# A softmax-times-V kernel: each row's product made for its two heads apart, in two halves of the PSUM partitions

## The chip, the cores and the metric

The kernel runs on one core of one Trainium2 chip. The metric is the device time of one launch in microseconds; a comparison uses the median of several launches.

## The reference

```python
scores: (8, 12, 1024, 1024) float32     # batch, heads, queries, keys
v:      (8, 12, 1024, 64)  float32
attn = exp(scores - max(scores, -1)); attn = attn / (sum(attn, -1) + 1e-8)
out  = matmul(attn, v)                   # (8, 12, 1024, 64) float32
```

The scores are 403 MB and are read once; everything else is small beside them.

## The kernel before, in words

There are 96 heads (batch times heads). One pass of the hardware loop takes `AHEAD` = 4 of them, so the loop runs 24 times. Two heads make a tile of the loop body (`T` = 2, `K` = 2 tiles in a body). A tile is `s_bufs[k]`, 128 partitions by `R` = 16 rows by 1024 scores in float32 (8 MB): partitions 0 to 63 hold the first head, 64 to 127 the second, and each partition has 16 neighbouring queries of its head. "Row r" below means the 128 queries (64 of each head) that stand at place r of all partitions.

For every tile the function `heads` goes through its 16 rows:

- ACT (line 377) takes exp of two rows at a time (one at a time in the last half of the second tile, where `late` holds), without subtracting the maximum, and writes float16 into `p_nat` (eight buffers of two rows, which is one whole tile).
- PE (line 390) transposes the row with 8 matmuls against the identity, one for each chunk of 128 keys, into `psT` in PSUM (two buffers of two rows).
- DVE (line 402, or 398 where `late` holds) copies `psT` to `pt` in SBUF.
- PE (line 152, function `finish`) makes the product with V: 8 matmuls, one for each chunk, which accumulate. The stationary operand is the 128x128 block of `pt` (64 queries of the one head, 64 of the other). The moving operand is V of both heads side by side with a column of ones, 130 columns in all (`M`). So all 128 queries are multiplied with both heads' V, and half of what comes out is not used.
- For each group of `G` = 3 rows (one PSUM bank, `psO`), DVE (function `normalise`) takes the reciprocal of the column of ones' result (line 132) and multiplies the 64 results with it, once for each head (line 140, partitions 0 to 63 and 64 to 127), into `out_bufs[k]`. The sixteenth row is a group of its own, so there are six groups in a tile.

`finish` runs `LAG` = 3 rows behind the transposes: the order on PE is written out by `in_line` as transposes of row r, product of row r-3, transposes of row r+1 and so on. At the end of a body the remaining products follow, and then `judge`: four small DVE instructions over the sums seen so far, one small matmul (line 297) and a cast. It decides whether a general path must run at the very end (it does not here). `watch_v` (line 259) is one DVE reduction over V in each body.

All transfers stand in one queue on SP in an order of their own (`queue`): the next body's first tile (`load_first`, behind ACT's reading of this body's first tile), the first tile's output, the next body's second tile, the second tile's output, and V two bodies ahead (behind GpSimd's spreading of V, line 248). In the last body the second tile is loaded in smaller pieces, and the function `end` stores the output in two parts.

Every weight load and every matmul of the body increments one semaphore of PE when it is done; DVE, ACT, GpSimd and SP wait on its value.

Of the kernel before, what the change touches and what calls it, by code (L numbers as in the profile page):

```python
# [12 lines left out]
ALU = mybir.AluOpType  # L13
# [13 lines left out]
def kernel(  # L27
# [6 lines left out]
    nc = tc.nc  # L34
    P = 128

    B, H, SQ, SK = scores.shape
    Bv, Hv, SKv, D = v.shape
# [2 lines left out]
    assert SQ % P == 0 and SK % P == 0  # L41
    C = SK // P
    EB = 2
    G = 3
    LAG = 3
    AHEAD = 4
    Q = P // AHEAD
# [5 lines left out]
    T = 2  # L53
    K = AHEAD // T
    W = P // T
    R = SQ // W
    N = D + 2
    M = T * N - 2
    GROUPS = -(-R // G)

    sc_rows = scores.rearrange("b h (j r) k -> (b h j) r k", j=W).rearrange(
        "(m x) r k -> m x r k", x=P
# [13 lines left out]
    vones = const_pool.tile([P, K, C, T, N], FP16, name="vones")  # L76
    nc.vector.memset(vones[:, :, :, :, D:N], 1.0)  # L77

    def buffers(pool, count, shape, dtype, name):
        return [pool.tile(shape, dtype, name=f"{name}{k}") for k in range(count)]  # L80
# [5 lines left out]
    out_bufs = buffers(sb_pool, K, [P, R, D], FP32, "out_sb")  # L86
    small_pool = ctx.enter_context(tc.tile_pool(name="small", bufs=1))
    seen = small_pool.tile([P, 1 + K * R + 1], FP32, name="seen")
# [7 lines left out]
    def take(bufs):  # L96
        k = turn.get(id(bufs), 0)
        turn[id(bufs)] = k + 1
        return bufs[k % len(bufs)]

    pending = []
# [3 lines left out]
    def after(a, b):  # L105

        tc.add_manual_dep(
            a.ins,
            b.ins.name,
            mybir.DependencyInfo(mybir.DependencyClass.NoSync, mybir.DependencyReason.DATA),  # L110
            reason="order",
        )

    def in_line(op):

        if line:
            after(op, line[-1])
        line.append(op)
# [4 lines left out]
            after(dma, queued[-1])  # L123
        queued.append(dma)

    def invert(k, st, g):

        rows = min(G, R - g * G)
        psO = st["psO"][g][:, 0 : rows * M].rearrange("p (g m) -> p g m", m=M)
        at = 1 + k * R + g * G  # L130
        recip = seen[:, at : at + rows].rearrange("p (g o) -> p g o", o=1)
        nc.vector.reciprocal(out=recip, in_=psO[:, :, D : D + 1])  # L132
        return psO, recip

    def normalise(k, st, g):
        psO, recip = invert(k, st, g)
        rows = min(G, R - g * G)
        for t in range(T):
            part = slice(t * W, (t + 1) * W)
            nc.vector.tensor_tensor(  # L140
                out=out_bufs[k][part, g * G : g * G + rows, :],
                in0=psO[part, :, t * N : t * N + D],
                in1=recip[part].to_broadcast([W, rows, D]),
                op=ALU.mult,
            )

    def finish(u):

        n0, k, r, pt, st = u
        g, i = r // G, r % G  # L150
        for c in range(C):
            product = nc.tensor.matmul(  # L152
                out=st["psO"][g][:, i * M : (i + 1) * M],
                lhsT=pt[:, c * P : (c + 1) * P],
                rhs=vones[:, k, c].rearrange("p t n -> p (t n)")[:, 0:M],
                start=(c == 0),
                stop=(c == C - 1),
            )
            in_line(product)
        if i == G - 1 or r == R - 1:  # L160
            normalise(k, st, g)
        if r == R - 1 and k < K - 1:
            spread_v(k)
            store(n0, k)

    def store(n0, k):

        to = out_rows.rearrange("(m x) y -> m x y", x=P)[bass.ds((n0 + T * k) // T, 1)]
        to = to.rearrange("o x y -> (o x) y")
        send(nc.sync.dma_start(out=to, in_=out_bufs[k][:].rearrange("x r d -> x (r d)")))  # L170

    def send(dma):
        for other in stores:
            apart(dma, other)
            apart(other, dma)
        apart(dma, dma)
        stores.append(dma)
        queue(dma)

    def end():  # L180

        cut = (GROUPS - 2) * G
        for a, b in ((0, cut), (cut, R)):
            send(
                nc.sync.dma_start(
                    out=out_rows[(BH - T) * W : BH * W, a * D : b * D],
                    in_=out_bufs[K - 1][:, a:b].rearrange("x r d -> x (r d)"),
                )
            )
# [8 lines left out]
    def rewrite(buf, op):  # L198


        others = writers.setdefault(buf.name, [])
        for other in others:
            apart(op, other, "readers in between")
            apart(other, op, "readers in between")
        apart(op, op, "readers in between")
        others.append(op)

    def other_bank(tile, bank, op):

        for other in users.setdefault((tile.name, 1 - bank), []):  # L210
            apart(op, other, "banks are disjoint")
            apart(other, op, "banks are disjoint")
        users.setdefault((tile.name, bank), []).append(op)
# [30 lines left out]
    def spread_v(k):  # L244

        for t in range(T):
            for s in range(S):
                spread = nc.gpsimd.tensor_copy(  # L248
                    out=vones[s * Q : (s + 1) * Q, k, :, t, 0:D].rearrange(
                        "i (h l) d -> i h l d", l=L  # L250
                    ),
                    in_=v_sb[(k * T + t) * Q : (k * T + t + 1) * Q, :, s],
                )
                for watch in watches:
                    apart(spread, watch, "products in between")

    def watch_v(behind):

        watch = nc.vector.tensor_reduce(  # L259
            out=most,  # L260
            in_=vones[:, :, :, :, 0:D].rearrange("p k c t d -> p k (c t) d"),
            axis=mybir.AxisListType.XYZ,
            op=ALU.max,
            apply_absolute_value=True,
        )
        after(watch, behind)
        watches.append(watch)
        for bound, op in ((V_MIN, ALU.is_ge), (V_MAX, ALU.is_le)):
            nc.vector.scalar_tensor_tensor(  # L269
                out=fits, in0=most, scalar=bound, in1=fits, op0=op, op1=ALU.mult  # L270
            )
# [9 lines left out]
    def judge(bank):  # L281
# [12 lines left out]
        )  # L294
        cell = bank[0:1, G * M : G * M + 1]
        in_line(
# [70 lines left out]
    def heads(n0):  # L367

        for k in range(K):
            st = dict(psO=[take(psO_bufs) for g in range(GROUPS)])  # L370
            for r in range(R):
                late = k == K - 1 and r >= R // 2
                if r % EB == 0:
                    p_nat, psT2, pt2 = take(p_bufs), take(psT_bufs), take(pt_bufs)
                    rows = 1 if late else EB
                    for g in range(0, EB, rows):
                        exp = nc.scalar.activation(  # L377
                            out=p_nat[:, g : g + rows, :].rearrange(
                                "p r (x v) -> p x r v", v=Q * L
                            ),  # L380
                            in_=s_bufs[k][:, r + g : r + g + rows, :].rearrange(
                                "p r (i x l) -> p x (r i) l", i=Q, l=L
                            ),
                            func=EXP,
                        )
                        rewrite(p_nat, exp)
                p_row = p_nat[:, r % EB, :].rearrange("p (h q l) -> p h l q", q=P, l=L)
                psT, pt = psT2[:, r % EB, :], pt2[:, r % EB, :]
                for c in range(C):
                    turned = nc.tensor.transpose(  # L390
                        out=psT[:, c * P : (c + 1) * P],
                        in_=p_row[:, c // L, c % L, :],
                        identity=ident16[:],
                    )
                    in_line(turned)
                    other_bank(psT2, r % EB, turned)
                if late:
                    copy = nc.vector.tensor_copy(out=pt, in_=psT)  # L398
                    rewrite(pt2, copy)
                    other_bank(psT2, r % EB, copy)  # L400
                elif r % EB == EB - 1:
                    copy = nc.vector.tensor_copy(out=pt2[:], in_=psT2[:])  # L402
                    rewrite(pt2, copy)
                if k == 0 and r == R // 2 - 1:
                    watch_v(copy)
                if r == R - 1 and k < K - 1:
                    load_first(n0)
                pending.append((n0, k, r, pt, st))
                if len(pending) > LAG:
                    finish(pending.pop(0))  # L410
        while pending:
            finish(pending.pop(0))
        last(n0)
        judge(st["psO"][-1])
# [51 lines left out]
```

## Time and profile before

| | |
|---|---|
| median of 3 runs | 1070.41 us (1070.23 to 1070.44) |
| the profiled execution: its time, its span | 1069.46 us, 1067.5 us |
| PE matmul busy | 793.6 us (74%), 12312 instructions |
| DVE busy | 768.8 us (72%), 1539 instructions |
| ACT busy | 737.3 us (69%) |
| transfers | 453.06 MB, mean 424 GB/s |
| one body of the loop, from the trace | 43.6 us |

Busy times of PE are of overlapping instructions, so the sum of a group says little of its pace; the starts in the timeline do. A name such as `L152` is line 152 of the kernel. PE stands for matmuls, PEld for weight loads.

### The profile page before, as it was taken

To read this page: it belongs to the slowest core of one execution; us is meant where nothing else is said; L and a number is where in the kernel's file an instruction comes from. 1 tells how busy PE (TensorE), PEld (TensorE's weight loads), DVE (VectorE), ACT (ScalarE), POOL (GpSimd) and SP (SyncE) were. 2 spreads that over 40 slices of the span, in tenths; PEclk is the share of its full clock that TensorE was granted. 3 is DMA by queue.
4 is the path that set the end of the run, shared out by engine and by line. 5 is a ranking of instruction groups with operands and counts; after the bars stand their busy time and mean duration, and the time that the engine had idled before them with its cause. 6 is when DMAs were issued, how large, how long until landed. Compare 5 with 4: busy or idle time off the path is not lost.

```text
span 1067.5 us, 32791 instructions
## 1 busy us (share of the span) xinstructions
PE 793.6 (74%) x12312; PEld 757.7 (71%) x12312; DVE 768.8 (72%) x1539; ACT 737.3 (69%) x504; POOL 239.2 (22%) x399
## 2 busy tenths in 40 slices
PE   2578768786786777867878668776786777866887
PEld 2578668686686776867768668776686777866877
DVE  1578767696686866867769667785686866867788
ACT  3567568666686576856867668667686586756893
POOL 3031131211311203113121131221311303113121
PEclk9889889898898988989989889898898988989899
DMA  9999999999999999999999999999999999999993
GB/s 393 441 438 413 422 462 413 452 413 431 453 413 452 426 419 449 417 433 446 440 425 449 425 423 452 413 428 456 413 452 413 431 453 413 452 410 434 432 429 151
DMA packets 18580, 453.06 MB, mean 424 GB/s; under 512 B 2064, under 2 KB 2192, under 8 KB 8720
## 3 DMA queue, kind: packets, MB, share of 16 engines
q1 hardware_dynamic: 18576, 452.99, 98.6%
q8 instruction: 4, 0.07, 0.0%
HBM read 637.53 MB, written 25.17 MB: 621 GB/s over the span
## 4 chain that ended last, share of the span: by engine, by line
DMA 58%; ACT 27%; issue 6%; PE 3%; PEld 2%; DVE 2%; ACTq 1%; SPq 0%; PEldq 0%; DVEq 0%
DMA s_nat<-in_scores_dram 58%; ACT p_nat L377 26%; PE psO L152 1%; PEld L390 1%; PE psT L390 1%; DVE pt L402 1%; PEld L152 1%; ACTq L377 1%; DVE most L259 0%; ACT L377 0%; DVE pt L398 0%; SPq L219 0%; ACTq L423 0%; DVE seen L132 0%; DVE out_sb L140 0%
## 5 line engine op out<-in xcount | busy, mean ns | idle before, releaser
L377 ACT ACTIVATE p_nat<-s_nat 128x2048 f16<-128x2048 f32 (+1 forms) x480 | 706.5, 1557 | 118.9 <-PE psO L152 42.5
L390 PE MATMUL psT<-ident,p_nat 128*128 128x128 f16 x6144 | 505.4, 232 | 166.2 <-ACT p_nat L377 166.2
L390 PEld LDWEIGHTS <-p_nat 128*128 128x128 f16 x6144 | 425.1, 118 | 176.0 <-ACT p_nat L377 176.0
L402 DVE COPY pt<-psT 128x2048 f16<-128x2048 f16 x288 | 352.4, 1224 | 261.5 <-PE L390 165.2
L152 PE MATMUL psO<-vones,pt 128*128 128x130 f16 x6144 | 486.6, 223 | 62.9 <-DVE fits L269 40.4
L152 PEld LDWEIGHTS <-pt 128*128 128x128 f16 x6144 | 387.8, 99 | 84.7 <-DVE pt L402 55.6
L248 POOL CAST vones<-v_sb 32x512 f16<-32x512 f32 x392 | 238.5, 608 | 813.4 <-PE psT L390 318.6
L140 DVE TENSOR_TENSOR out_sb<-psO,seen 64x192 f32<-64x192 f32 (+1 forms) x576 | 191.8, 333 | 18.0
L377 ACT ACT_TABLE_LOAD x24 | 30.8, 1283 | 195.4 <-DMA s_nat<-in_scores_dram 178.5
L398 DVE COPY pt<-psT 128x1024 f16<-128x1024 f16 x192 | 123.5, 685 | 2.3
L259 DVE TENSOR_REDUCE most<-vones 128x1 f32<-128x2048 f16 x24 | 54.9, 2286 | 0.7
L132 DVE RECIPROCAL seen<-psO 128x3 f32<-128x3 f32 (+1 forms) x288 | 49.3, 171 | 2.8 <-PE L390 1.4
L297 PE MATMUL psO<-vones,right 128*1 128x1 f16 x24 | 3.9, 164 | 41.0 <-DVE right L292 41.0
L297 PEld LDWEIGHTS <-right 128*1 128x1 f16 x24 | 1.9, 79 | 45.3 <-DVE right L292 45.3
L301 DVE CAST count<-psO 1x1 int32<-1x1 f32 x24 | 3.5, 146 | 6.2 <-PE psO L297 6.2
L269 DVE SCALAR_TENSOR_TENSOR fits<-most,fits 128x1 f32<-128x1 f32 x48 | 7.4, 155 | 0.0
L289 DVE SCALAR_TENSOR_TENSOR part<-seen,fits 128x1 f32<-128x1 f32 x24 | 5.3, 220 | 0.8
L285 DVE TENSOR_REDUCE seen<-seen 128x1 f32<-128x33 f32 x24 | 4.5, 188 | 0.8
L292 DVE SCALAR_TENSOR_TENSOR right<-seen,part 128x1 f16<-128x1 f32 x24 | 3.9, 162 | 0.8
L286 DVE TENSOR_REDUCE seen<-seen 128x1 f32<-128x33 f32 x24 | 4.2, 177 | 0.0
L77 DVE MEMSET vones<- 128x64 f16 x1 | 0.1, 112 | 0.8 <-PEq L450 0.8
L74 DVE CAST ident<-ident 128x128 f16<-128x128 f32 x1 | 0.2, 227 | 0.4 <-POOL ident masks.py:199 0.4
(8 smaller groups left out, 1.1 us busy)
## 6 DMA issues: line engine op xcount, KB each, us to landing
s_nat<-in_scores_dram SPq DMA_DIRECT2D x50, 4096.0 KB, 18.7
v_sb<-in_v_dram SPq DMA_DIRECT2D x24, 1024.0 KB, 22.2
out_dram<-out_sb SPq DMA_DIRECT2D x47, 512.0 KB, 16.8
s_nat<-in_scores_dram SPq DMA_DIRECT2D x2, 2048.0 KB, 22.8
s_nat<-in_scores_dram SPq DMA_DIRECT2D x1, 1536.0 KB, 27.5
s_nat<-in_scores_dram SPq DMA_DIRECT2D x3, 512.0 KB, 20.8
s_nat<-in_scores_dram SPq DMA_DIRECT2D x1, 1024.0 KB
s_nat<-in_scores_dram SPq DMA_DIRECT2D x47, 28.4
```

The source lines that it names most:

```text
L132: nc.vector.reciprocal(out=recip, in_=psO[:, :, D : D + 1])
L140: nc.vector.tensor_tensor(out=out_bufs[k][part, g * G : g * G + rows, :], in0=psO[part, :, t * N : t * N + D], in1=recip[part].to_broadcas ...
L152: product = nc.tensor.matmul(out=st["psO"][g][:, i * M : (i + 1) * M], lhsT=pt[:, c * P : (c + 1) * P], rhs=vones[:, k, c].rearrange("p t ...
L248: spread = nc.gpsimd.tensor_copy(out=vones[s * Q : (s + 1) * Q, k, :, t, 0:D].rearrange("i (h l) d -> i h l d", l=L), in_=v_sb[(k * T + t) ...
L259: watch = nc.vector.tensor_reduce(out=most, in_=vones[:, :, :, :, 0:D].rearrange("p k c t d -> p k (c t) d"), axis=mybir.AxisListType.XYZ, ...
L269: nc.vector.scalar_tensor_tensor(out=fits, in0=most, scalar=bound, in1=fits, op0=op, op1=ALU.mult)
L289: nc.vector.scalar_tensor_tensor(out=part, in0=seen[:, n + 1 : n + 2], scalar=1.0, in1=fits, op0=ALU.is_le, op1=ALU.mult)
L297: nc.tensor.matmul(out=cell, lhsT=right[:], rhs=vones[:, 0, 0, 0, D : D + 1], start=True, stop=True)
L377: exp = nc.scalar.activation(out=p_nat[:, g : g + rows, :].rearrange("p r (x v) -> p x r v", v=Q * L), in_=s_bufs[k][:, r + g : r + g + ro ...
L390: turned = nc.tensor.transpose(out=psT[:, c * P : (c + 1) * P], in_=p_row[:, c // L, c % L, :], identity=ident16[:],)
L398: copy = nc.vector.tensor_copy(out=pt, in_=psT)
L402: copy = nc.vector.tensor_copy(out=pt2[:], in_=psT2[:])
```

## The change

The product of a row is made by 16 matmuls instead of 8: for each chunk and each head one, with 64 columns of `pt` as stationary operand and that head's own 65 columns of V and ones as moving operand. The first head's result goes to PSUM partitions 0 to 63, the second's to 64 to 127. The tiles that the build gives to these instructions are 128x64 at columns 0 and 64 of the array; transposes keep 128x128. A row now takes 65 columns of PSUM instead of 130, so a bank holds four rows (`G` = 4), a tile has four groups, and one multiplication of 128 partitions by 256 elements normalises a group. Near the end of a body (`late`, the last two rows) the products run two rows behind instead of three. In the built program the body has 256 weight loads and 256 matmuls for transposes as before, and 512 and 512 instead of 256 and 256 for products; the order of DVE, ACT, GpSimd and SP instructions is the same but for the fewer normalisations.

```diff
-    G = 3
+    G = 4
...
-    M = T * N - 2
-    GROUPS = -(-R // G)
+    M = D + 1
+    GROUPS = R // G
...
-    def invert(k, st, g):
-
-        rows = min(G, R - g * G)
-        psO = st["psO"][g][:, 0 : rows * M].rearrange("p (g m) -> p g m", m=M)
+    def normalise(k, st, g):
+
+        psO = st["psO"][g][:, 0 : G * M].rearrange("p (g m) -> p g m", m=M)
         at = 1 + k * R + g * G
-        recip = seen[:, at : at + rows].rearrange("p (g o) -> p g o", o=1)
+        recip = seen[:, at : at + G].rearrange("p (g o) -> p g o", o=1)
         nc.vector.reciprocal(out=recip, in_=psO[:, :, D : D + 1])
-        return psO, recip
-
-    def normalise(k, st, g):
-        psO, recip = invert(k, st, g)
-        rows = min(G, R - g * G)
-        for t in range(T):
-            part = slice(t * W, (t + 1) * W)
-            nc.vector.tensor_tensor(
-                out=out_bufs[k][part, g * G : g * G + rows, :],
-                in0=psO[part, :, t * N : t * N + D],
-                in1=recip[part].to_broadcast([W, rows, D]),
-                op=ALU.mult,
-            )
+        nc.vector.tensor_tensor(
+            out=out_bufs[k][:, g * G : (g + 1) * G, :],
+            in0=psO[:, :, 0:D],
+            in1=recip.to_broadcast([P, G, D]),
+            op=ALU.mult,
+        )
...
         for c in range(C):
-            product = nc.tensor.matmul(
-                out=st["psO"][g][:, i * M : (i + 1) * M],
-                lhsT=pt[:, c * P : (c + 1) * P],
-                rhs=vones[:, k, c].rearrange("p t n -> p (t n)")[:, 0:M],
-                start=(c == 0),
-                stop=(c == C - 1),
-            )
-            in_line(product)
-        if i == G - 1 or r == R - 1:
+            for t in range(T):
+                product = nc.tensor.matmul(
+                    out=st["psO"][g][t * W : (t + 1) * W, i * M : (i + 1) * M],
+                    lhsT=pt[:, c * P + t * W : c * P + (t + 1) * W],
+                    rhs=vones[:, k, c, t, 0:M],
+                    start=(c == 0),
+                    stop=(c == C - 1),
+                )
+                in_line(product)
+        if i == G - 1:
             normalise(k, st, g)
...
-        cut = (GROUPS - 2) * G
+        cut = (GROUPS - 1) * G
...
-                if len(pending) > LAG:
+                while len(pending) > (LAG - 1 if late and r >= R - EB else LAG):
                     finish(pending.pop(0))
```

## The prediction, made before the changed kernel ran

> **What bounds the kernel now.** I read the page first, then the windows of one body and of the end, then the timeline of one body, then the list of waits, and last the trace's own record of semaphore updates.
>
> ```profile
> q1 hardware_dynamic: 18576, 452.99, 98.6%
> L390 PE MATMUL psT<-ident,p_nat 128*128 128x128 f16 x6144 | 505.4, 232 | 166.2 <-ACT p_nat L377 166.2
> L152 PE MATMUL psO<-vones,pt 128*128 128x130 f16 x6144 | 486.6, 223 | 62.9 <-DVE fits L269 40.4
> 505.10:548.70 43.60, 32.54 (x513) 30.98 (x513) 32.00 (x64) 30.77 (x22) 10.97 (x19) 0.90 1.00 433
> 1048.00:1068.00 20.00, 13.31 (x226) 12.72 (x223) 14.79 (x38) 3.62 (x4) 4.78 (x8) 0.93 0.16 62
> ```
>
> The first three are lines of the page, the last two windows (length, busy time of PE, PEld, DVE, ACT, POOL, clock, DMA share, GB/s). For a body of 43.6 us the DMA engines are never idle: transfers set the period, and PE, DVE and ACT each have about 11 us to spare. Only in the last 20 us are the transfers over; there the time is that of the chain through PE and DVE.
>
> ```profile
> 513.42 0.61 PE L390 MATMUL psT<-ident,p_nat 128*128 128x128 f16 x8
> 513.87 0.62 PE L152 MATMUL psO<-vones,pt 128*128 128x130 f16 x8
> 514.16 1.22 DVE L402 COPY pt<-psT 128x2048 f16<-128x2048 f16 x1 [0.84 <-PE psO L152]
> 514.33 0.61 PE L390 MATMUL psT<-ident,p_nat 128*128 128x128 f16 x8
> ...
> 502.13 0.64 PE L152 MATMUL psO<-vones,pt 128*128 128x130 f16 x8 [0.74 <-DVE pt L398]
> ...
> 504.48 0.17 PE L297 MATMUL psO<-vones,right 128*1 128x1 f16 x1 [1.71 <-DVE right L292]
> ...
> 508.36 3.70 PE L390 MATMUL psT<-ident,p_nat 128*128 128x128 f16 x32 [3.72 <-ACT p_nat L377]
> ```
>
> In the timeline a row takes PE 0.91 us (513.42 to 514.33): 8 transposes 0.45, 8 products 0.46, that is 55 to 57 ns for a weight load and its matmul. A body has 32 rows, 29.1 us. Then PE waits, for `judge` (1.71) and for the next tile (3.72).
>
> ```profile
> DVE pt L402 <- PE L152: 48.8, 35, 11.3
> DVE pt L402 <- PE psO L152: 42.9, 45, 1.8
> ```
>
> These are the lines of the list of waits that I find odd. The copy at L402 needs transposes (L390), yet it is mostly released while products run; the copy at 514.16 starts 0.13 us after the transposes' modelled end. The record of semaphore updates says why. PE's semaphore gets 24,629 increments, one from each of the 12,312 weight loads and 12,312 matmuls and a few more. Of the 24,628 distances between them, 23,208 are exactly 30 ns, and none is shorter. In busy stretches 36 instructions end in a microsecond and 33 increments come; the increments fall up to 22 behind the ends, and DVE starts 23 to 24 ns after an increment, not after an end. So PE's done signals go out one by one, 30 ns each. A row now has 32 of them, 0.96 us, just over PE's 0.91; a body 1026 of them, 30.8 us, well under 43.6.
>
> **The change, part by part.**
>
> *Signals.* A row gets 16 transposing instructions (8 loads, 8 matmuls) and 32 for the product, each with its increment: 48 x 30 ns = 1.44 us. A body has 512 + 1024 + 2 = 1538, and 1538 x 0.030 = 46.1 us, more than the 43.6 us of the transfers. This alone makes PE's signals the bound, whatever the matmuls cost up to 1.44 us a row.
>
> *PE itself.* No instruction of 64 stationary columns stands in the trace. Below: the moving columns halve (65 for 130), so a load and matmul take 27.5 ns and the row stays at 0.91. Above: they take 55 ns, as the fullest ones do, 16 x 55 = 0.88, and the row is 1.33. The array also changes between tiles of 128 and 64 columns twice a row. A change costs nothing if it is hidden; at most it waits for the last matmul (about 220 ns from start to end, less the usual 55) and a load (97 ns), 0.26 us. So a row takes PE 0.91 to 1.86 us. I take 1.15 to 1.4, in the middle, below the signals' 1.44, and keep the upper end for the range.
>
> [...]
>
> *DVE.* The multiplications of a tile go from 10 of 64x192 (355 ns) and 2 of 64x64 (222) to 4 of 128x256. The two rows give 133 ns for 128 elements more, so 64x256 would be about 422; all partitions work at once. With 6 and 4 reciprocals of 0.17: 5.0 us becomes 2.4 a tile, 5.2 us saved a body. It lies beside PE and the transfers and is worth nothing in the steady bodies. PE's wait of 1.7 us a body behind `watch_v` (40.4 us over 24 bodies, put down to DVE fits in the L152 line above) goes too: at 1.44 us a row, the signals of two rows (2.88) outlast the reduction (2.29), and the copy behind it is needed only two rows later.
>
> *Lag.* One product moves ahead of the last transposes. At the end of a body it covers the last copy (0.69 us; 0.74 of wait at 502.13 is gone). This I count as part of the signal stream.
>
> *What follows at the body's end.* Signals stop from the last product's increment (502.80) to the next body's first (now 508.49). What stays of that when PE no longer waits for a tile: reciprocal, multiplication, four small ones and the small matmul to 504.66 (1.86; the new multiplication costs 0.42 for 0.47), PE's branch rows to 505.58 (0.92), then the first load's 0.13: 2.9 us. Then four rows of transposes (64 signals, 1.92) stand against the first two rows' 0.96, copy 1.24 and about 0.2 of starts, so 0.45 us more. Together 3.4.
>
> So a body takes 46.1 + 3.4 = 49.5 us.
>
> *Who waits for it.* Transposes free `p_nat` more slowly, so ACT reads the first tile later, and `load_first` also stands in SP's queue behind the V load, which follows GpSimd's spread (5.3 us after the last product). It is issued about 3 us into a body and needs some 22 us; the tile is then read by transposes that begin at 49.5. The second tile is issued at about 26, behind the first tile's store, and lands at about 47. Neither is late. DMA has 5.9 us of idle in a body.
>
> *Sum.* In the first body the second tile is landed for row 16 at 47.69, as before; 16 rows of transposes and 19 of products are left: (256 + 608) x 0.030 = 25.9 us, last signal at 73.7. Then 23 bodies of 49.5 = 1138.5: last signal at 1212.2. From the last signal to the end of the span it was 1061.93 to 1067.5, 5.6: span 1217.8. The profiled execution's time was 1.96 above its span, and the median 0.95 above that: 1220.7.
>
> **Rivals.**
>
> *PE is slower still.* Row 1.44 to 1.86. Each 0.1 us of a row is 3.2 us a body and 75 us in all. With 55 ns for each load and matmul and 0.16 lost at each change of tile, a row is 1.65, a body 56.3, the time about 1385; with both upper ends it is 1535. For it: 64 columns take as long to load as anything the trace bounds. Against: the moving columns halve. It decides where a row passes 1.44.
>
> *The signals do not hold PE* (the two halves' signals go out faster than 30 ns, or the pace belongs to profiled executions alone). Then up to a row of 1.26 (43.6 less 3.4, by 32) transfers go on hiding it, and only the last body, where PE's chain ends last, pays 32 times the row's growth: 0.1 us is 3 us; from 1070 to 1085. Between 1.26 and 1.44 it rises to 1215. Against: DVE's starts follow the paced increments, and profiled and timed executions differ by 0.1%.
>
> *Faster.* The two heads' halves run side by side in the array, 30 ns for both, and their signals keep up with less than 60 ns for a chunk. Then a row falls under 0.91, the last body's chain shortens, and DVE's saving cuts its waits (1.7 after `watch_v`). With the row at 0.91 that and the lag give about 2 us, 1068; with a row at 0.70 the end is held by ACT's last exp at 1051.6, 8 us better, 1062. [...] It needs signals at least twice as fast as the fastest recorded.
>
> **How the numbers follow.** Signals set the body: 0.53 (1190 to 1240, as the 3.4 us may be 2.2 to 4.2). PE slower still: 0.25. Signals do not hold: 0.14, of which 0.05 within 0.2%. Faster: 0.08. A difference of 0.2% is what a measurement of this kernel surely tells from none. Slower is 0.53 + 0.25 + 0.09 = 0.87. The range goes from 1090 to 1470: it leaves out the faster case, most of the hidden one and the uppermost part of the slow one, together 0.2.
>
> **What would show it.** The body's period 49.5 us; PE's increments at 30 ns almost without gaps but for 3.4 us a body; DVE busy near 645 us; DMA share about 88%; ACT waiting for PE's transposes and no longer for transfers. If matmul starts in the timeline show a row of over 1.44 with increments keeping up, PE itself is slower; if the DMA row stays at 98%, the signals did not hold. A jump of the instruction queue's 0.07 MB would mean that the longer body is fetched again, which I have not priced.

## The result and the profile after

The changed kernel takes 1246.81 us (1246.62 to 1246.92, 6 runs); the kernel before, run beside it, 1070.32 (1068.57 to 1070.94, 6 runs). The ratio is 1.165 (95% interval 1.164 to 1.167): slower by 176.5 us. The prediction was 1220.7, within 1090 to 1470.

First the page of the changed kernel (the queue's row, then groups: line, engine, operation, count | busy us, mean ns | idle time before them) and a window of about one body.

```profile
span 1244.7 us, 44479 instructions
...
q1 hardware_dynamic: 18576, 452.99, 87.5%
...
L145 PE MATMUL psO<-vones,pt 128*64 128x65 f16 x12288 | 620.3, 197 | 46.0 <-DVE pt L395 20.4
L383 PE MATMUL psT<-ident,p_nat 128*128 128x128 f16 x6144 | 519.6, 235 | 49.7 <-ACT p_nat L370 27.2
```

```profile
500.00:551.20 51.20, 45.03 (x783) 40.05 (x781) 27.94 (x45) 32.27 (x23) 9.77 (x16) 0.93 0.88 369
```

The same bytes go through the queue, but the DMA engines are now idle an eighth of the time: transfers no longer set the pace. PE has twice the product matmuls, its group's busy time grew from 486.6 us only to 620.3, and DVE is busy for 28 us of a body.

In the list of waits (engine and line, what it waited for: us in total, times, longest) ACT and DVE now wait for PE:

```profile
ACT p_nat L370 <- PE L145: 141.1, 199, 4.8
DVE pt L395 <- PE L145: 128.0, 103, 7.6
DVE pt L391 <- PE L145: 106.4, 143, 0.8
...
PE psT L383 <- ACT p_nat L370: 27.2, 2, 20.2
...
ACT p_nat L370 <- DMA s_nat<-in_scores_dram: 13.0, 1, 13.0
```

PE waited for ACT 47 times before (166.2 us), and now twice, both in the first body: the next tile no longer holds PE up. The list seems to say that ACT no longer waits for transfers either (178.5 us, 22 times, before its table load in the kernel before). Here the list misleads:

```profile
509.97 1.28 ACT L370 ACT_TABLE_LOAD   x1 [5.63 <-PE psT L383]
511.26 9.12 ACT L370 ACTIVATE p_nat<-s_nat 128x2048 f16<-128x2048 f32 x5
```

By the record of landings, 22 of these table loads start 89 or 90 ns after the last piece of a tile's transfer has landed, as 22 did before the change (88 or 89). ACT still waits 5.1 to 8.4 us for a transfer there. The list names PE because an increment of PE comes every 30 ns, so one is nearly always the latest event. The wait costs nothing now: this tile is transposed from 532.86 on, some 20 us after ACT's first rows of it are ready.

The copies at L391 and L395 need transposes (L383) but are released "by" products, as before, and now for longer. The timeline of the late rows says how much longer:

```profile
516.85 0.64 PE L383 MATMUL psT<-ident,p_nat 128*128 128x128 f16 x8
...
518.29 0.64 PE L383 MATMUL psT<-ident,p_nat 128*128 128x128 f16 x8
518.86 0.94 PE L145 MATMUL psO<-vones,pt 128*64 128x65 f16 x16
519.11 0.69 DVE L391 COPY pt<-psT 128x1024 f16<-128x1024 f16 x1 [0.75 <-PE L145]
519.73 0.64 PE L383 MATMUL psT<-ident,p_nat 128*128 128x128 f16 x8
```

A row takes 1.44 us (518.29 to 519.73), which is 48 x 30 ns. The copy at 519.11 takes the row whose transposes ended at 517.49: it starts 1.62 us later, after 0.75 us in which DVE was idle. The record of semaphore updates has 36,917 increments of PE's semaphore; 36,011 of the distances are 30 ns, one is 29, none shorter. In full flow some 55 instructions have ended whose increments are still to come: a queue of signals. It never gets longer than 58, and when it is about that long PE starts its loads and matmuls one by one, each 30 ns after the last.

While this queue still has room, PE shows what it could do. Near the start of a body (23 signals queued at 538.17, 38 at 539.11):

```profile
538.17 0.64 PE L383 MATMUL psT<-ident,p_nat 128*128 128x128 f16 x8
538.73 0.33 PEld L145 LDWEIGHTS <-pt 128*64 128x64 f16 x16
538.73 0.44 PE L145 MATMUL psO<-vones,pt 128*64 128x65 f16 x16
...
539.11 0.64 PE L383 MATMUL psT<-ident,p_nat 128*128 128x128 f16 x8
```

Sixteen loads and sixteen matmuls in 0.44 us: a row of 0.94 us (538.17 to 539.11), hardly more than the 0.91 of before. The product for two heads apart is as quick on PE as the joint one. Its done signals are not.

### The profile page after: what moved, and what is told of

Read it like the earlier page. It is cut to its first block, busy times and chain, and to the rows that moved or that the text cites. A ratio compares the mean times of both kernels' runs of the same rounds, so it can differ in the third digit from the quotient of the medians.

```text
span 1244.7 us, 44479 instructions
## 1 busy us (share of the span) xinstructions
PE 1066.4 (86%) x18456; PEld 949.1 (76%) x18456; DVE 666.0 (54%) x1059; ACT 765.7 (62%) x504; POOL 240.2 (19%) x399
## 3 DMA queue, kind: packets, MB, share of 16 engines
q1 hardware_dynamic: 18576, 452.99, 87.5%
## 4 chain that ended last, share of the span: by engine, by line
PEld 49%; DVE 26%; issue 10%; PE 6%; DMA 4%; another core or an unknown queue 2%; PEldq 1%; ACT 0%; SPq 0%; DVEq 0%
PEld L145 32%; DVE pt L395 22%; PEld L383 17%; PE psT L383 5%; DMA s_nat<-in_scores_dram 4%; DVE pt L391 2%; PE psO L145 2%; DVE seen L131 1%; ACT p_nat L370 0%; DVE part L282 0%; PEldq L416 0%; PEldq L346 0%; PE psO L290 0%; DVE seen L278 0%
## 5 line engine op out<-in xcount | busy, mean ns | idle before, releaser
L370 ACT ACTIVATE p_nat<-s_nat 128x2048 f16<-128x2048 f32 (+1 forms) x480 | 734.9, 1565 | 302.1 <-PE L145 141.1
L145 PE MATMUL psO<-vones,pt 128*64 128x65 f16 x12288 | 620.3, 197 | 46.0 <-DVE pt L395 20.4
L145 PEld LDWEIGHTS <-pt 128*64 128x64 f16 x12288 | 538.8, 109 | 130.0 <-DVE pt L395 63.1
L383 PE MATMUL psT<-ident,p_nat 128*128 128x128 f16 x6144 | 519.6, 235 | 49.7 <-ACT p_nat L370 27.2
L395 DVE COPY pt<-psT 128x2048 f16<-128x2048 f16 x288 | 351.5, 1221 | 256.4 <-PE L145 128.0
L383 PEld LDWEIGHTS <-p_nat 128*128 128x128 f16 x6144 | 408.4, 121 | 80.3 <-ACT p_nat L370 27.5
L391 DVE COPY pt<-psT 128x1024 f16<-128x1024 f16 x192 | 132.6, 691 | 107.1 <-PE L145 106.4
L131 DVE RECIPROCAL seen<-psO 128x4 f32<-128x4 f32 x192 | 35.4, 184 | 192.7 <-PE L383 132.6
L370 ACT ACT_TABLE_LOAD x24 | 30.8, 1283 | 145.7 <-PE L383 49.6
L132 DVE TENSOR_TENSOR out_sb<-psO,seen 128x256 f32<-128x256 f32 x192 | 81.3, 423 | 9.7 <-DVE seen L131 4.7
L282 DVE SCALAR_TENSOR_TENSOR part<-seen,fits 128x1 f32<-128x1 f32 x24 | 11.3, 469 | 0.8
```

The costliest lines, as they stand in the source:

```text
L132: nc.vector.tensor_tensor(out=out_bufs[k][:, g * G : (g + 1) * G, :], in0=psO[:, :, 0:D], in1=recip.to_broadcast([P, G, D]), op=ALU.mult,)
L145: product = nc.tensor.matmul(out=st["psO"][g][t * W : (t + 1) * W, i * M : (i + 1) * M], lhsT=pt[:, c * P + t * W : c * P + (t + 1) * W], ...
L282: nc.vector.scalar_tensor_tensor(out=part, in0=seen[:, n + 1 : n + 2], scalar=1.0, in1=fits, op0=ALU.is_le, op1=ALU.mult)
L370: exp = nc.scalar.activation(out=p_nat[:, g : g + rows, :].rearrange("p r (x v) -> p x r v", v=Q * L), in_=s_bufs[k][:, r + g : r + g + ro ...
L383: turned = nc.tensor.transpose(out=psT[:, c * P : (c + 1) * P], in_=p_row[:, c // L, c % L, :], identity=ident16[:],)
```

## The experiments

**The theories.** Signals: PE's increments leave one per 30 ns, and 1538 of them make a body. Tiles: changing between tiles of 128 and 64 columns and loading 64 columns cost PE the time. Matmuls: PE's own work on twice the products does.

**Run signals: the signals alone, added to the kernel before.**

```diff
                 start=(c == 0),
-                stop=(c == C - 1),
+                stop=False,
             )
             in_line(product)
+            product = nc.tensor.matmul(
+                out=st["psO"][g][:, i * M + D + 1 : i * M + D + 2],
+                lhsT=pt[:, c * P : (c + 1) * P],
+                rhs=vones[:, k, c, 0, D + 1 : D + 2],
+                start=False,
+                stop=(c == C - 1),
+            )
+            in_line(product)
```

> The kernel before, with 8 more matmuls of one moving column in every row's product: the same stationary blocks of 128 columns, result added into a column that nothing reads. A row has 48 increments of PE's semaphore as the changed kernel has, but no 64-column tiles and no change of tile size. Signals theory (increments go out one per 30 ns and hold PE): a body takes 1538 x 0.030 = 46.1 us and 4 to 4.5 us of gaps, the time is 1235 to 1250. Tile theory (the changes between 128- and 64-column tiles and the 64-column loads cost PE the time): PE's row is 0.91 + 8 x 0.03 = 1.15 us, transfers hide it, 1070 to 1080.

Measured: 1252.1 us, ratio 1.171 (1.169 to 1.173). A body takes 50.85 us. Its page shows the added group beside the old one:

```profile
L152 PE MATMUL psO<-vones,pt 128*128 128x130 f16 x6144 | 702.8, 219 | 54.4 <-DVE pt L410 25.4
L160 PE MATMUL psO<-vones,pt 128*128 128x1 f16 x6144 | 660.9, 165 | 0.0
```

Eight loads and eight matmuls of one column a row, with the old product and the old tile size, cost as much as the whole change. Tiles are not needed for it. While the queue has room a row takes PE 1.12 us there (500.12 to 501.24 in its timeline). Once it is full, loads and matmuls start one every 30 ns:

```profile
503.54 0.10 PEld L152 LDWEIGHTS <-pt 128*128 128x128 f16 x1
503.57 0.22 PE L152 MATMUL psO<-vones,pt 128*128 128x130 f16 x1
503.60 0.10 PEld L160 LDWEIGHTS <-pt 128*128 128x128 f16 x1
503.63 0.16 PE L160 MATMUL psO<-vones,pt 128*128 128x1 f16 x1
```

The time is 2 us above the upper end of what was expected, as gaps are 4.7 us a body.

**Run half: the change with half of its products.**

```diff
         for c in range(C):
-            for t in range(T):
+            for t in (c % T,):
...
-                    start=(c == 0),
-                    stop=(c == C - 1),
+                    start=(c < T),
+                    stop=(c >= C - T),
```

> The changed kernel with every second matmul of the products left out: the first head takes the even chunks of keys, the second the odd ones, so each result sums half of its keys. Tiles of 64 columns, their loads and two changes of tile size a row stay; increments fall from 48 to 32 a row, as before the change. Signals theory: a body's signals are 30.8 us, transfers bind again, 1066 to 1075. Tile theory: the two changes of tile size a row stay and cost about as much as in the changed kernel; PE's row falls by 8 half-width matmuls, 0.22 to 0.44 of 1.44 us, and the time is 1075 to 1180.

Measured: 1069.2 us, ratio 0.9993 (0.9984 to 1.0003), no difference from the kernel before. The queue is at its old share (page), and a row takes PE 0.82 us (timeline, 523.14 to 523.96):

```profile
q1 hardware_dynamic: 18576, 452.99, 98.6%
```

```profile
523.14 0.64 PE L383 MATMUL psT<-ident,p_nat 128*128 128x128 f16 x8
523.71 0.20 PEld L145 LDWEIGHTS <-pt 128*64 128x64 f16 x8
523.71 0.32 PE L145 MATMUL psO<-vones,pt 128*64 128x65 f16 x8
523.96 0.48 PEld L383 LDWEIGHTS <-p_nat 128*128 128x128 f16 x8
```

The tile changes are all there: transposes take 0.57 us from their first start to the product's, where they took 0.45 in the kernel before. So the change to the smaller tiles costs about 0.1 us, and at 32 signals a row transfers hide it. The same run has the four-row groups and the faster normalisation, and gains nothing by them.

**Run wide: nearly twice the moving columns.**

```diff
-    M = D + 1
+    M = 126
...
-                    rhs=vones[:, k, c, t, 0:M],
+                    rhs=vones[:, k, c].rearrange("p t n -> p (t n)")[:, 0:M],
```

> The changed kernel with 126 moving columns in place of 65 for each product matmul (both heads take the first head's V, so the second head's result is not its own). Increments stay at 48 a row. Signals theory: PE's own row grows from about 0.94 to at most 1.4 us, under the signals' 1.44, and the time stays, 1244 to 1265. Matmul theory (PE's own work sets the row's 1.44 us): 16 x 61 columns more are up to 0.4 us a row, 13 us a body, 1500 to 1550.

Measured: 1259.95 us, ratio 1.178 (1.176 to 1.180); a body takes 51.2 us for 50.65. While the queue has room a row is 1.13 us (503.65 to 504.78 in its timeline; 0.94 with 65 columns):

```profile
503.65 0.64 PE L383 MATMUL psT<-ident,p_nat 128*128 128x128 f16 x8
...
504.22 0.63 PE L145 MATMUL psO<-vones,pt 128*64 128x126 f16 x16
...
504.78 0.64 PE L383 MATMUL psT<-ident,p_nat 128*128 128x128 f16 x8
```

PE's own row grew by 0.19 us, which over 32 rows is 6 us a body; the body grew by 0.5. The signals cover the rest. Matmul work is not what sets the row.

**Runs signals40 and signals44: where the bound takes over.** The kernel before with 4 and 6 of the one-column matmuls a row instead of 8 (the loop goes on to the next chunk where `c` is 4 or 6 and more).

```diff
                 start=(c == 0),
                 stop=(c == C - 1),
             )
             in_line(product)
+            if c >= 4:
+                continue
+            product = nc.tensor.matmul(
+                out=st["psO"][g][:, i * M + D + 1 : i * M + D + 2],
+                lhsT=pt[:, c * P : (c + 1) * P],
+                rhs=vones[:, k, c, 0, D + 1 : D + 2],
+                start=False,
+                stop=False,
+            )
+            in_line(product)
```

> The kernel before with 4 matmuls of one column more in a row (as in the run with 8): 40 increments a row, 1282 in a body, 38.5 us. With the 4.7 us of gaps that the run with 8 showed (50.85 - 46.14) a body would take 43.2, just under the 43.6 of the transfers. Signals theory: hidden in all bodies but the last, where 32 rows grow by 0.24 us: 1070 to 1080. Rival (each added instruction costs its part of the 182 us, half of 8): 1150 to 1165.

> The same with 6 matmuls more in a row: 44 increments a row, 1410 in a body, 42.3 us, and 4.7 of gaps: 47.0 us a body. Signals theory: 23 x (50.85 - 47.0) and 2.3 in the first body less than the 1252.1 of the run with 8: 1161, between 1150 and 1172. Rival (proportional): 1207. Another rival (only PE's own pace counts, 0.91 and 6 x 0.03): 1070 to 1078.

Measured: 1099.1 us (ratio 1.028, 1.026 to 1.029) and 1162.9 (1.087, 1.086 to 1.089). With 44 the body is 46.9 us as worked out. With 40 it is 44.4, not 43.2: signals are 38.5 and the gaps 5.9, not 4.7. The window of that run still has the DMA share at 1.00:

```profile
500.00:543.60 43.60, 36.27 (x628) 35.02 (x626) 32.95 (x64) 30.70 (x21) 9.00 (x16) 0.92 1.00 433
```

Yet transfers do not hold this body. ACT has the first rows of a tile ready well before PE turns to them, and PE's waits are for DVE:

```profile
463.08 14.52 ACT L387 ACTIVATE p_nat<-s_nat 128x2048 f16<-128x2048 f32 x8
...
473.41 3.58 PE L400 MATMUL psT<-ident,p_nat 128*128 128x128 f16 x32 [1.01 <-DVE count L311]
...
487.40 0.23 PE L152 MATMUL psO<-vones,pt 128*128 128x130 f16 x1 [1.49 <-DVE fits L279]
```

From the second body on ACT's first rows are done 1.5 us or more before PE's first transposes. In the record of increments, signals stop behind the reduction over V (0.28 us at 487) and for 2.24 us at the body's end, where with 44 signals a row it is 1.77. So with fewer signals queued, more of PE's own waits show. What else makes up the 1.2 us more of gaps was not taken apart.

So at 40 signals PE's own body (44.4) is already just above that of the transfers (43.6), and my expectation, which took the gaps from the run with 8, missed by 19 us above its upper end. From 32 to 40 signals a row the body grows by 0.8 us, where 256 signals of 30 ns are 7.7; from 40 to 44 it grows by 2.6 and from 44 to 48 by 3.9, where 128 signals are 3.8. Past the crossing the time goes up with the signals; before it, transfers hide them. The proportional rivals (1150 to 1165 for 40, 1207 for 44) are out.

**Runs nojudge and warm: the gaps of a body.** The prediction had 3.4 us of gaps; the trace has 4.5 (50.65 less 46.14). The timeline at a body's end:

```profile
528.02 0.44 PE L145 MATMUL psO<-vones,pt 128*64 128x65 f16 x16 [0.54 <-DVE pt L391]
530.15 0.18 DVE L131 RECIPROCAL seen<-psO 128x4 f32<-128x4 f32 x1 [2.19 <-remote]
...
531.75 0.16 PE L290 MATMUL psO<-vones,right 128*1 128x1 f16 x1 [3.29 <-DVE right L285]
...
532.86 3.57 PE L383 MATMUL psT<-ident,p_nat 128*128 128x128 f16 x32 [0.94 <-DVE count L294]
```

The last product ends at 528.46 on PE. The reciprocal, put down to an unknown releaser, waits until 530.15 for its signal, the last in the queue (recorded at 530.13). PE stands still until 531.75, and at 532.86 the 32 first transposes take 3.57 us, 107 ns each: the record of the granted clock is at half from 530.76 on for 6.83 us. Two runs take the gap apart.

```diff
         last(n0)
-        judge(st["psO"][-1])
```

(`count` is set once, ahead of the loop.)

> The changed kernel without the judgement at the end of a body (four small DVE instructions, one small matmul, one cast), so the decision on the general path is left out. A body of the changed kernel takes 50.63 us, of which the signals are 46.14 and 4.49 are gaps: 2.9 from the last product's signal to the next body's first, about 1.6 more at the body's start, where the clock is at half. Clock theory: PE goes on to the next transposes while its signals are still queued, the pause of 4.4 us and the half clock go, and a body takes 46.4 to 47.2 us: 1150 to 1170. Rival (the 1.6 us at the start are the first copies' wait, whatever the clock): only the 2.9 go, 47.7 us, about 1180.

```diff
+        for d in range(12):
+            in_line(
+                nc.tensor.matmul(
+                    out=psO_bufs[0][:],
+                    lhsT=ident16[:],
+                    rhs=vones[:, 0].rearrange("p c t n -> p (c t n)")[:, 0:512],
+                    start=True,
+                    stop=True,
+                )
+            )
         last(n0)
         judge(st["psO"][-1])
```

> The changed kernel with 12 more matmuls of 512 moving columns (identity by V, into a PSUM bank that is free then, never read) behind the last product of a body: 2.6 us of PE work in the pause in which PE waits for the judgement, 24 more signals that go out in that pause. Clock theory: PE is no longer idle for 4.4 us, the clock stays at full, the 32 transposes at the start take 1.8 to 2.1 us and not 3.57, a body is 1.0 to 1.3 us shorter: 1216 to 1225. Rival (the start's 1.6 us are not the clock's): 1246 to 1252.

Measured: nojudge 1163.4 us (ratio 1.088, 1.086 to 1.090), a body of 47.0; warm 1223.2 (1.144, 1.142 to 1.146), a body of 49.6. The first transposes of a body, nojudge and then warm:

```profile
544.43 1.95 PE L384 MATMUL psT<-ident,p_nat 128*128 128x128 f16 x32 [0.78 <-issue]
```

```profile
519.56 2.76 PE L408 MATMUL psO<-vones,ident 128*128 128x512 f16 x12
...
524.01 1.95 PE L383 MATMUL psT<-ident,p_nat 128*128 128x128 f16 x32 [0.94 <-DVE count L294]
```

Both take 1.95 us for the same 32 transposes, 1.62 less. In warm nothing else changed, and 24 signals more were added: useless work for PE makes the kernel some 23 us faster, 1.0 us a body, and its record of the clock has no half inside the loop after the first body (mean granted clock 0.995, for 0.931 in the changed kernel). There PE's pause is 4.4 us (528.46 to 532.86), broken only by the small matmul at 531.75; in 23 passes of its loop the clock falls 0.3 to 3.6 us after the last product has ended (2.3 at 530.76), so the time from that end to the fall differs from pass to pass. In nojudge the next body starts while signals are still queued, and of 4.5 us of gaps 0.9 is left.

**Run lag: the new lag alone, on the kernel before.**

```diff
-                if len(pending) > LAG:
+                while len(pending) > (LAG - 1 if late and r >= R - EB else LAG):
```

> The kernel before with the changed line on the lag alone: in the last two rows of a body the products run two rows behind. One product of 0.46 us moves ahead of the last transposes and covers the wait for the last copy (0.74 us). Theory: transfers hide it in all bodies but the last, where PE's chain ends last; 0.3 to 0.6 us faster, about 1069.9. Rival: the last row's transposes start later by the product that now stands ahead of them, and its copy with them; no change.

Measured: ratio 0.9999 (0.999 to 1.0008), spans 1067.5 and 1067.5: no difference. The rival's account (the last transposes are pushed back by the product ahead of them) fits, but is not shown.

**What no run separates.** In all of these kernels every load and every matmul of the body increments the semaphore. That PE can start instructions much faster than one per 30 ns is shown (32 within 0.38 us while the queue has room), so it is what follows an instruction's end that takes 30 ns. Whether that is the increment, or something that every instruction does on its way out, could be told by a kernel in which only the instructions that someone waits for increment. No run has that.

## Why the prediction was right, and where it was off

- *Signals set the body.* Right, and shown from both sides: instructions with their increments, added without the change, give its time (signals), and taken from the change they give back the old one (half). The 30 ns read from the trace of before held: 36,011 of the 36,916 distances after the change, one start per 30 ns in signals (503.54 to 503.63), and 3.9 us a body for 128 signals between the runs with 44 and 48.
- *PE's own row*, taken at 1.15 to 1.4, was too high: 0.94 while the queue has room. The halves of the two heads do run side by side, 16 of each kind in 0.44 us, as the faster rival had it, and the change to the smaller tiles costs about 0.1 us (0.57 for 0.45 in half), not up to 0.26. The rival fails by its own second condition: the signals of a chunk take 120 ns, not under 60. The slower rival, with a row over 1.44, did not come about.
- *The gaps of a body* were mis-sized: 3.4 us predicted, 4.5 measured. The end of the body was right (2.9 predicted; from the last product's signal at 530.13 to the next body's first at 532.96 it is 2.83). The start was wrong: transposes at full clock and 0.45 us for the copy, 2.4 together; it took 3.5, as the clock was at half. The trace of before showed it (32 transposes in 3.70 us at 508.36, the line quoted in the prediction), but the sum counts these transposes at 30 ns a signal. 23 bodies of 1.15 us more are 26 us, the whole difference between 1220.7 and 1246.8; warm, with the clock at full there, gets some 23 of them back. The rest of the sum held: the first body's last signal is at 74.6 us (73.7 predicted), and 5.4 us follow the last product's signal (5.6).
- *DVE.* The multiplication took 423 ns (422 estimated), and multiplications and reciprocals together fell by 124.4 us, 5.2 a body, as worked out. DVE's busy time fell to 666 and not 645: the late copies took 132.6 us for 123.5 (L391) and one instruction of the judgement 11.3 for 5.3 (L282); the rest, some 6 us, was not traced. Worth nothing here, as said.
- *The wait behind the reduction over V* is not wholly gone: 0.59 us is left where the first products after it wait for their copy (547.09 in the timeline), for 1.7.
- *Lag.* The wait of 0.74 us for the last copy is not gone, as the prediction had it: 0.54 is left (528.02). It costs nothing, since signals are still going out then.
- *Who waits.* The DMA share went to 87.5% (88% forecast), and from the second body on PE no longer waits for a tile. The instruction queue moved 0.10 MB for 0.07, in 7 packets over the 24 passes: the body was not fetched on every pass. That ACT would no longer wait for transfers was wrong: it still waits for each body's first tile, as shown above, but nothing waits for ACT there.

## What to carry to other kernels

Count PE's done signals as a resource of its own: here each load and each matmul, all of which increment a semaphore, took 30 ns of a single line, so splitting a matmul into two smaller ones doubled that price even where the two started within 5 ns of each other. The sign is a consumer that the list of waits puts down to a later instruction than the one it needs. With a signal every 30 ns the list can also put a wait for a transfer down to PE, and a DMA share of 1.00 did not mean, with 40 signals a row, that transfers set the pace: look at what the late engine itself waits for. And in a loop whose end makes PE wait, look at the first matmuls of the next pass: filling the pause with useless matmuls took 1.6 us off them and 1.0 us off a body here, and leaving the judgement out of the loop gave 83 us.

## What the runs showed that I had not expected

The queue of signals did not grow past 57 or 58 instructions over and unsignalled in the changed kernel's trace (22 or 23 in the kernel before). Well below that number PE ran at its own pace there (a row of 0.94 us at 538.17), and near it at that of the signals (1.44 us at 518.29). At the end of a body the last reciprocal starts 1.69 us after the last product's end (528.46 to 530.15), and 1.70 in nojudge and in warm (543.65 to 545.35, 519.62 to 521.32). In the row of 0.94 us the matmuls of two 64-column halves start within 5 ns of each other. The half kernel, with PE's row at 0.82 us, ends no sooner than the kernel before with 0.91, though PE's chain ends last there: both have 32 signals a row, 0.96 us, which would explain it. No run takes signals away from the last body alone, so that is argued and not shown.
